# Seven products in another order, fewer loads ahead, and rearranged last rows in a hybrid decoder layer

## The chip, the cores and the metric

The kernel runs on one core of a Trainium2 chip. The metric is the device time of one execution in microseconds (us), the median of several runs. The engines are TensorE (PE; PEld is its weight load), VectorE (DVE), ScalarE (ACT), GpSimd (POOL) and SyncE (SP), which here only issues DMAs. Each engine works through a queue of its own in order; semaphores order them among each other.

## What is computed

A decoder layer on 1024 tokens of width 1024, in float32. First comes a token-mixing sub-layer (attention and a gated recurrence, one output projection), which the change doesn't touch. Then comes the channel-mixing sub-layer, which is more than half of the time:

```python
h = rmsnorm(x, pre_w_mlp[l]) * (1.0 + sc2) + sh2
u = jnp.square(jax.nn.relu(h @ w_up[l]))          # 1024 x 4096
x = x + g2 * rmsnorm(u @ w_down[l], post_w_mlp[l])
```

sh2, sc2 and g2 are rows made from a conditioning vector. The gate row g2 times the norm weight is `gw2` in the kernel.

## The kernel before, in words

**Products.** Each float32 operand is split into a high part (a rounded copy, made by ScalarE) and a low part (the difference, made by VectorE); a product of two operands is three matmuls, high by high, high by low, low by high. Every matmul has 128 rows of weights and 512 columns.

**The up scheme.** The hidden width is cut into 32 blocks of 128; two blocks are a pair, so there are 16 pairs (`NG`). Pairs 0 and 1 are computed directly (`load_cl`, `up_cl`, lines 1250 to 1264). For pairs 2 to 15 the four quarter products are built from seven products instead of eight, numbered 1 to 7, as in Strassen's scheme. Each product needs sums of the four blocks of `w_up` (`a11`, `a12`, `a21`, `a22`; `wsum`, `whi` for the high part, `wlo` for the low part) and a factor of the tokens (`bt[n, kt]`, four tiles; 5, 6, 7 and 4 are differences, made once by `factor`, line 1021; 1, 2, 3 and 8 are the tokens themselves). A product is 12 matmuls (`prod`, line 1114). Products 1, 6, 7 and 4 add up in one bank "a", 5 and 3 in bank "c", 2 in bank "b". Between them ScalarE copies the bank's state out (`snap`) and VectorE adds it to another bank (`merge`); a copy has to be done before the next product adds into the same bank. Then come `relu2` (two ScalarE operations) and sums of the results (`usum`), which are stored to `ud` in DRAM, since the down phase uses the same scheme.

**Order in the loop.** `up_slot(p, k)`, line 1305, writes out by hand what is issued in slot k of pair p; `ORDER_UP` has the order of products 1, 5, 4, 6, 3, 2, 7, where 4 is the one of the pair before. ScalarE, VectorE, TensorE and SP are "pinned": their instructions run in the order in which they are written. Elsewhere, and for GpSimd here, a planner chooses the order. In the first pair, p0 = 2, the factors of product 4 are made in slots 1 to 4 (line 1379). GpSimd makes sums of `w_dn` blocks for the down phase (`down_sums`, stored to `td`) and, for pairs 0 and 1, of their results (`direct_sums`); `JOBS` has one of them for each pair.

**The border.** The down phase reads a list `seq` of entries: `entry_w` (a `w_dn` block or `td`) and `entry_u` (`ud`), in turn; for each, a load by SP, a high part on ScalarE and a low part on VectorE. `load_ahead` (line 1227) issues loads up to `LEAD` = 6 entries ahead of the one in use; `pump(n)` splits the next n. In the last pair's slots 2 to 6 it splits 2, 3, 3, 3 and 3 entries (line 1387); the first two down stages (products 1 and 5 of pairs 0 to 3) have 8 entries each. The last pair's product 4 and the merge ahead of it (`u_tail`, line 1453) are done in the first down stage, between its four products of 128 tokens. Stores wait in `pend` until `flush` issues them on SP, at the start of a slot, in line with the loads. Loads take buffers in turn from two pools (`raw_`, 3, and `t_`, 5).

**The end.** In the last down group (pairs 14 and 15) the steps finish the rows of tokens one after the other: `accum` (VectorE), `square` (ScalarE), `root` (three GpSimd operations on a column of 128 sums), `gated` (times `gw2`, GpSimd), `scaled` (times the root, ScalarE), `residual` (plus x, VectorE), each at a step number given by `on`. `last_rows` (line 1548) does the last two blocks of rows, 3 and 7, of which 7 is finished last: its last half comes from the product `bx` ("pdlx"), in two halves of 256 columns.

## Time and profile before

| what | us |
|---|---|
| runs: lowest, median, highest | 1141.04, 1142.5, 1143.09 |
| the profiled execution: its own time | 1137.53 |
| its span, first to last instruction | 1135.7 |
| TensorE busy in the span | 1079.2 |
| VectorE, ScalarE, GpSimd busy | 825.6, 597.8, 411.3 |

All times of the trace are counted from the start of the span. "Idle before" is the time in which an engine had nothing to do ahead of an instruction, with what ended it; the profile infers that from semaphores. The pairs 2 to 15 of the up scheme run from 531 to 800 us, the down phase from there to 1119 us.

### The profile page before, as it was taken

How to read it: one execution, taken by the hardware profiler on the slowest of the kernel's cores; microseconds unless marked ns; L12 is line 12 of the kernel's file. 1: busy time of each engine (PE TensorE's matmuls, PEld its weight loads, DVE VectorE, ACT ScalarE, POOL GpSimd, SP SyncE). 2: the span in 40 equal slices, each digit the busy share in tenths (PEclk: the TensorE clock that was granted, in tenths of full speed). 3: DMA queues.
4: the chain of work that ended last, by engine and by line, in shares of the span. 5: the costliest groups of instructions: out<-in, count | busy, mean ns of one | idle time of the engine just before them, and what ended most of it. 6: DMA issues, size and time to landing. Idle time of an engine off the chain costs nothing.

```text
span 1135.7 us, 16039 instructions
## 1 busy us (share of the span) xinstructions
PE 1079.2 (95%) x5392; PEld 880.9 (78%) x5392; DVE 825.6 (73%) x1337; ACT 597.8 (53%) x1232; POOL 411.3 (36%) x534
## 2 busy tenths in 40 slices
PE   4899999999999999999899999999899999999994
PEld 3788766788788788887788888888688888888873
DVE  4865777878865564549876777887767676998786
ACT  5454654264465654565555555555664543654343
POOL 3444221134224653427555564555343000000155
PEclk9899999999999999999999999999999999999997
DMA  9700400634410343314688787777998565986554
GB/s 340 265 10 1 149 1 2 194 114 130 131 57 1 120 150 111 121 66 144 223 265 279 256 288 257 261 256 248 328 379 280 194 213 181 315 267 203 166 172 162
DMA packets 104259, 207.30 MB, mean 183 GB/s; under 512 B 13808, under 2 KB 14576, under 8 KB 104176
## 3 DMA queue, kind: packets, MB, share of 16 engines
q1 hardware_dynamic: 90288, 161.18, 41.9%
q0 software_dynamic: 13600, 44.58, 11.8%
q8 instruction: 42, 0.69, 0.2%
q10 hardware_dynamic: 288, 0.52, 0.1%
q14 instruction: 41, 0.34, 0.1%
HBM read 151.17 MB, written 55.05 MB: 182 GB/s over the span
## 4 chain that ended last, share of the span: by engine, by line
PE 78%; DVE 8%; DMA 5%; ACT 4%; POOL 3%; issue 2%; SPq 0%; DVEq 0%; POOLq 0%; ACTq 0%
PE pda L39 14%; PE pua L39 13%; PE po L39 7%; PE pdc L39 7%; PE puc L39 6%; PE pdb L39 3%; PE pv L39 3%; PE phg L39 3%; PE phq L39 3%; PE pub L39 3%; PE pq L39 3%; PE phf L39 3%; PE pu L39 2%; DMA wa<-wada 2%; PE pk L39 1%
## 5 line engine op out<-in xcount | busy, mean ns | idle before, releaser
L39 POOL TENSOR_TENSOR b<-b,b 128x512 f32<-128x512 f32 x64 | 98.8, 1544 | 81.0 <-DMA b<-w_dn 80.4
L39 ACT ACTIVATE dw<-dwr 128x512 fp32r<-128x512 f32 x72 | 45.3, 629 | 46.7 <-DMA dwr<-td 26.0
L39 ACT ACTIVATE s<-s 128x512 f32<-128x512 f32 x84 | 53.0, 631 | 31.0 <-DVE s L39 29.6
L1441 POOL DMA_DIRECT2D b<-b_g x2 | 1.1, 540 | 187.7 <-DVE acc L39 187.5
L39 DVE TENSOR_TENSOR acc<-pda,acc 128x512 f32<-128x512 f32 x68 | 46.7, 687 | 25.3 <-PE pda L39 24.2
L39 DVE TENSOR_TENSOR dw<-dwr,dw 128x512 fp32r<-128x512 f32 x72 | 55.2, 766 | 2.2 <-ACT dw L39 2.2
L39 POOL DMA_DIRECT2D b<-w_dn x64 | 34.5, 541 | 47.2 <-DMA td<-b 44.3
L39 POOL DMA_DIRECT2D td<-b x64 | 35.9, 562 | 21.6 <-POOL b L39 18.7
L39 DVE TENSOR_TENSOR wt<-a,wt 128x512 fp32r<-128x512 f32 x42 | 40.1, 955 | 0.0
L39 ACT ACTIVATE s<-pua 128x512 f32<-128x512 f32 x28 | 16.7, 597 | 42.2 <-PE pua L39 30.0
L39 PE MATMUL pua<-bt_0h,wt 128*128 128x512 f32 x84 | 32.9, 392 | 4.2 <-ACT s L39 4.2
L39 ACT ACT_TABLE_LOAD x28 | 35.9, 1283 | 0.5
L39 DVE SCALAR_TENSOR_TENSOR macc<-wada,cs,macc 128x512 f32<-128x512 f32 x42 | 33.6, 799 | 2.3 <-DMA wada<-wada 1.7
L39 DVE TENSOR_TENSOR acc<-pdc,acc 128x512 f32<-128x512 f32 x36 | 24.8, 688 | 13.5 <-PE pdc L39 13.0
L39 POOL TENSOR_TENSOR comb<-comb,rd 128x512 f32<-128x512 f32 x8 | 11.7, 1459 | 63.3 <-DVE rd L39 44.2
L39 DVE TENSOR_TENSOR wt<-s,wt 128x512 fp32r<-128x512 f32 x42 | 33.4, 794 | 0.7 <-ACT wt L39 0.6
L39 PE MATMUL pua<-bt_1h,wt 128*128 128x512 f32 x84 | 32.7, 389 | 0.0
L39 PE MATMUL pua<-bt_2h,wt 128*128 128x512 f32 x84 | 32.7, 389 | 0.0
L39 PE MATMUL pua<-bt_3h,wt 128*128 128x512 f32 x84 | 32.7, 389 | 0.0
L39 PE MATMUL pda<-dw,du_6h 128*128 128x512 f32 x96 | 29.8, 392 | 1.1 <-DVE acc L39 1.1
L39 ACT ACTIVATE wt<-s 128x512 fp32r<-128x512 f32 x42 | 26.3, 627 | 7.7 <-DVE s L39 7.5
L39 PE MATMUL pdc<-dw,du_3h 128*128 128x512 f32 x96 | 29.7, 390 | 0.2 <-DVE acc L39 0.2
(751 smaller groups left out, 3816.9 us busy)
## 6 DMA issues: line engine op xcount, KB each, us to landing
dur<-ud SPq DMA_DIRECT2D x112, 256.0 KB, 3.5
wada<-wada SPq DMA_DIRECT2D x64, 256.0 KB, 3.2
b<-w_dn POOLq DMA_DIRECT2D x64, 256.0 KB, 4.3
td<-b POOLq DMA_DIRECT2D x64, 256.0 KB, 3.3
dwr<-td SPq DMA_DIRECT2D x64, 256.0 KB, 3.6
a<-w_u SPq DMA_DIRECT2D x56, 256.0 KB, 4.4
dwr<-w_dn SPq DMA_DIRECT2D x48, 256.0 KB, 3.8
ud<-s SPq DMA_DIRECT2D x42, 256.0 KB, 3.9
```

What stands on the lines that cost most here:

```text
L39: ins = op(*args, **kw)
L1441: nc.gpsimd.dma_start(b5, I["b_g2"][hs[half]].partition_broadcast(P))
```

## The change

In the first pair the order of products becomes 1, 2, 5, 6, 3, (none), 7, and its product 4 is done after product 3 of the next pair. The loads and splits for its products 1 and 2 are written earlier; the factors of product 4 are made in slots 3 to 6, sums, high parts and low parts each a slot after the other. GpSimd is pinned in the loop too, with `direct_sums` first. The first 16 entries of `seq` are loaded 4 ahead instead of 6, and the last pair's slots 5 and 6 split 1 and 0 entries instead of 3 and 3. At the end, `root` becomes one VectorE and one GpSimd operation; the factor sqrt(D) that the root then lacks is put into `gw2`, whose multiplication goes to VectorE. `scaled` and `residual` move up one and two steps for rows 0, 1, 4 and 5; for rows 2 and 6 one fused operation on VectorE (`final`) does both. In `last_rows` the order of the last operations changes, and row 7's gated halves get tiles of their own (`gl`).

```diff
+    def factor_sum(n, kt):
         b11, b12, b21, b22 = raws[kt][0], raws[kt][1], raws[kt + 4][0], raws[kt + 4][1]
         dst, x, y = {5: (b11, b12, b11), 6: (b11, b22, b11), 7: (b12, b22, b12), 4: (b21, b21, b11)}[n]
         DVE.tensor_tensor(dst, x, y, ALU.subtract)
-        bt[n, kt] = split(dst, m_ if n == 4 else hT_, f"bt{n}_{kt}")
+        fraw[n, kt] = dst
+
+    def factor_hi(n, kt):
+        mk = m_ if n == 4 else hT_
+        fhl[n, kt] = hi, lo = mk(f"bt{n}_{kt}h", dt=F32R), mk(f"bt{n}_{kt}l", dt=F32R)
+        ACT.activation(hi, fraw[n, kt], AF.Copy)
+
+    def factor_lo(n, kt):
+        bt[n, kt] = hi, lo = fhl.pop((n, kt))
+        DVE.tensor_tensor(lo, fraw.pop((n, kt)), hi.bitcast(F32), ALU.subtract)
...
-        while at["load"] < min(len(seq), at["use"] + LEAD + 1):
+        while at["load"] < min(len(seq), at["use"] + (LEAD if at["load"] >= 16 else 4) + 1):
...
+    p0 = CL // 2
+    aload(p0, "a11", "a12", "a21", "a22")
+    whi(p0, 1)
+    wlo(p0, 1)
     for f in range(4):
         up_cl(f, 1)
-    p0 = CL // 2
     factors(5)
-    aload(p0, "a21", "a22", "a11", "a12")
+    whi(p0, 2)
+    wlo(p0, 2)
...
-    JOBS = [(down_sums, k) for k in range(4)] + [(direct_sums, k) for k in range(2)]
-    JOBS += [(down_sums, k) for k in range(4, 12)]
+    JOBS = [(direct_sums, k) for k in (1, 0)] + [(down_sums, k) for k in range(12)]
...
-        n = ORDER_UP[k]
+        n = ORDER_UP[k] if old else (1, 2, 5, 6, 3, None, 7)[k]
+        k4 = 4 if o == p0 else 2
         flush()
-        if k == 2:
-            if old:
-                prod(o, 4)
-        else:
+        if n and (k != 2 or not old):
             prod(p, n)
+        if old and k == k4:
+            prod(o, 4)
...
-    pin(True, ACT, DVE, PE, SP)
+    pin(True, ACT, DVE, POOL, PE, SP)
     for p in range(p0, NG):
         for k in range(7):
             up_slot(p, k)
-            if p == p0 and 1 <= k <= 4:
-                factor(4, k - 1)
+            if p == p0 and k >= 3:
+                for kt in (2 * k - 6, 2 * k - 5):
+                    if kt < 4:
+                        factor_sum(4, kt)
+                    if 2 <= kt < 6:
+                        factor_hi(4, kt - 2)
+                    if kt >= 4:
+                        factor_lo(4, kt - 4)
...
-                pump((0, 0, 2, 3, 3, 3, 3)[k], ends[1])
+                pump((0, 0, 2, 3, 3, 1, 0)[k], ends[1])
...
-                POOL.tensor_tensor(gw2[:, hs[half]], gw2[:, hs[half]], g5[half][3], ALU.mult)
+                DVE.scalar_tensor_tensor(gw2[:, hs[half]], gw2[:, hs[half]], float(D ** 0.5), g5[half][3], ALU.mult, ALU.mult)
...
+    def root_of(r, part, a, b):
+
+        DVE.tensor_scalar(part, a, b, D * EPS, ALU.add, ALU.add)
+        POOL.tensor_tensor(r, part, mhalf[:, 0:1], ALU.pow)
...
-                for j, hf in ((4, 1 - half), (5, half)):
+                for j, hf in ((3, 1 - half), (4, half)) if t < 2 else ():
                     on(step + j, lambda tb=tb, hf=hf: scaled(tb, hf))
-                for j, hf in ((6, 0), (7, 1)):
+                for j, hf in ((4, 0), (5, 1)) if t < 2 else ():
                     on(step + j, lambda tb=tb, hf=hf: residual(tb, hf))
...
+        def final(tb, half):
+            if (tb, 0) not in xs:
+                xs[tb, 0], xs[tb, 1] = take(), take()
+            DVE.scalar_tensor_tensor(accs[tb][half], accs[tb][half], rr_[tb][:, 0:1], xs[tb, half], ALU.mult, ALU.add)
+            store(tb, half)
...
         add(accs[b][1], ba)
+        sq(accs[b][1], ss[:, 0:1])
         add(accs[b][0], ba)
         root(a)
         gated(a, 1)
-        sq(accs[b][1], ss[:, 0:1])
-        scaled(a, 0)
-        for step in range(nstep + 3, max(later, default=0) + 1):
-            rest(step)
-        xa = [take(), take()]
...
-        DVE.tensor_tensor(accs[b][0], accs[b][0], gw2[:, h[0]], ALU.mult)
-        POOL.tensor_scalar(one["t"], ss[:, 2:3], one["part"][:, 0:1], 1.0 / D, ALU.add, ALU.mult)
-        POOL.tensor_tensor(one["r"], one["t"], mhalf[:, 0:1], ALU.pow)
-        DVE.tensor_tensor(accs[a][0], accs[a][0], xa[0], ALU.add)
+        DVE.tensor_tensor(gl[1], accs[b][1], gw2[:, h[1]], ALU.mult)
+        DVE.tensor_scalar(one["part"], ss[:, 0:1], ss[:, 1:2], D * EPS, ALU.add, ALU.add)
+        DVE.tensor_tensor(gl[0], accs[b][0], gw2[:, h[0]], ALU.mult)
+        DVE.tensor_tensor(one["part"], one["part"], ss[:, 2:3], ALU.add)
+        POOL.tensor_tensor(one["r"], one["part"], mhalf[:, 0:1], ALU.pow)
+        final(6, 1)
+        xa = [take(), take()]
+        for half in range(2):
+            scaled(a, half)
+            POOL.tensor_tensor(accs[a][half], accs[a][half], xa[half], ALU.add)
+        for half in range(2):
+            DVE.scalar_tensor_tensor(gl[half], gl[half], one["r"][:, 0:1], take(), ALU.mult, ALU.add)
+            (nc.scalar if half else nc.sync).dma_start(out[b * P:(b + 1) * P, h[half]], gl[half])
         store(a, 0)
+        final(6, 0)
```

## Rows read from the trace of the kernel before

**Rows 1.** The page: busy time of each engine, and two of its costliest groups.

```profile
PE 1079.2 (95%) x5392; PEld 880.9 (78%) x5392; DVE 825.6 (73%) x1337; ACT 597.8 (53%) x1232; POOL 411.3 (36%) x534
...
L39 ACT ACTIVATE dw<-dwr 128x512 fp32r<-128x512 f32 x72 | 45.3, 629 | 46.7 <-DMA dwr<-td 26.0
...
L39 DVE TENSOR_TENSOR dw<-dwr,dw 128x512 fp32r<-128x512 f32 x72 | 55.2, 766 | 2.2 <-ACT dw L39 2.2
```

**Rows 2.** What TensorE waited for, 470 to 1136: total us, times, longest.

```profile
PE pua L39 <- DVE s L39: 4.5, 1, 4.5
...
PE pua L39 <- ACT s L39: 4.2, 2, 2.4
...
PE pda L39 <- DVE acc L39: 1.3, 3, 0.7
```

**Rows 3.** Stretches: us, busy PE, PEld, DVE, ACT, POOL, clock, DMA share, GB/s.

```profile
835.00:1090.00 255.00, 254.05 (x1119) 209.45 (x1117) 201.15 (x312) 123.07 (x205) 21.89 (x26) 1.00 0.71 234
...
800.00:805.00 5.00, 5.00 (x24) 3.99 (x23) 4.30 (x8) 2.63 (x5) 1.76 (x3) 1.00 1.06 399
...
811.00:815.00 4.00, 4.00 (x11) 3.13 (x12) 3.66 (x4) 3.03 (x6) 2.76 (x3) 0.57 0.98 345
```

**Rows 4.** Timeline of TensorE, first pair: start, duration, [idle before <- releaser].

```profile
531.04 0.39 PE L39 MATMUL pua<-bt_0h,wt 128*128 128x512 f32 x1
...
533.76 0.39 PE L39 MATMUL puc<-bt_0h,wt 128*128 128x512 f32 x1
...
538.42 0.50 PE L39 MATMUL pua<-bt_0h,wt 128*128 128x512 f32 x1 [1.78 <-ACT s L39]
...
541.97 0.50 PE L39 MATMUL puc<-bt_0h,wt 128*128 128x512 f32 x1 [0.54 <-ACT s L39]
...
550.12 0.50 PE L39 MATMUL pua<-bt_0h,wt 128*128 128x512 f32 x1 [2.42 <-ACT s L39]
```

**Rows 5.** Timeline of the other engines ahead of and in the first pair.

```profile
521.12 2.26 DVE L39 TENSOR_TENSOR h<-h,h 128x512 f32<-128x512 f32 x1
...
521.52 1.30 POOL L39 TENSOR_TENSOR b<-b,b 128x512 f32<-128x512 f32 x1
...
548.96 0.63 ACT L39 ACTIVATE bt_2h<-h 128x512 fp32r<-128x512 f32 x1 [4.41 <-DVE h L39]
```

**Rows 6.** Timeline of SP, VectorE and TensorE at the border of the phases.

```profile
792.84 0.33 SPq L39 DMA_DIRECT2D dwr<-w_dn  x1
...
800.70 0.69 DVE L39 TENSOR_TENSOR us<-a,us 128x512 f32<-128x512 f32 x1 [4.88 <-DMA ud<-s]
...
808.07 1.00 DVE L39 TENSOR_TENSOR du_5l<-dur,du_5h 128x512 fp32r<-128x512 f32 x1 [1.87 <-ACT du_5h L39]
...
810.20 0.68 DVE L39 TENSOR_TENSOR s<-pua,s 128x512 f32<-128x512 f32 x1
...
810.93 0.50 PE L39 MATMUL pua<-bt_0h,wt_4h 128*128 128x512 f32 x1 [4.46 <-DVE s L39]
...
815.39 0.62 PE L39 MATMUL pda<-dw,du_1h 128*128 128x512 f32 x2
```

**Rows 7.** The chain that ended last, at the border: start, us, what.

```profile
793.23 7.03 DMA ud<-s
```

**Rows 8.** Timeline of all engines after the last product.

```profile
1118.24 0.40 PE L39 MATMUL pdlx<-dw,du_4h 128*128 128x256 f32 x2
...
1121.27 1.95 ACT L39 ACTIVATE acc<-acc,r_f 128x512 f32<-128x512 f32 x3 [2.40 <-POOL r_f L39]
...
1124.46 0.42 DVE L39 TENSOR_TENSOR acc<-pdlx,acc 128x256 f32<-128x256 f32 x1
...
1127.87 0.56 POOL L39 TENSOR_TENSOR l_r<-l_t,mhalf 128x1 f32<-128x1 f32 x1
...
1128.40 1.26 POOL L39 TENSOR_TENSOR acc<-acc,x 128x512 f32<-128x512 f32 x1
...
1128.46 2.41 DVE L39 SCALAR_TENSOR_TENSOR acc<-acc,l_r,x 128x512 f32<-128x512 f32 x2 [0.73 <-POOL l_r L39]
```

More of the change, by code (lines that the diff above doesn't have):

```diff
@@ L1019, in second_raw @@
             bt[n, kb % 4] = (hi, lo)
-    def factor(n, kt):
+    fraw, fhl = {}, {}
+    def factor_sum(n, kt):
         b11, b12, b21, b22 = raws[kt][0], raws[kt][1], raws[kt + 4][0], raws[kt + 4][1]
@@ L1024, in factor @@
         DVE.tensor_tensor(dst, x, y, ALU.subtract)
[L1025 removed]
+        fraw[n, kt] = dst
[6 more added lines that the diff above has]
+        DVE.tensor_tensor(lo, fraw.pop((n, kt)), hi.bitcast(F32), ALU.subtract)
     def factors(n):
         for kt in range(4):
[L1029 removed]
+            factor_sum(n, kt)
+            factor_hi(n, kt)
+            factor_lo(n, kt)
     for tb in range(5):
@@ L1290, in hybrid_layer @@
     wsum(p0, 6)
-    for n in (6, 2):
-        whi(p0, n)
-        wlo(p0, n)
+    whi(p0, 6)
+    wlo(p0, 6)
     wsum(p0, 3)
@@ L1330, in up_slot @@
         elif k == 2:
-            snap(p, "c", "s5")
             if old:
+                snap(p, "c", "s5")
                 usum(o, 5)
@@ L1339, in up_slot @@
             aload(q + 1, "a22")
-            if old:
+            if old and k4 == 2:
                 relu2_a12(o)
                 usum(o, 6)
+            elif not old:
+                snap(p, "c", "s5")
             if more:
@@ L1354, in up_slot @@
                 wsum(q, 6)
-            if old:
+            if old and k4 == 2:
                 usum(o, 3)
@@ L1359, in up_slot @@
         elif k == 5:
+            if old and k4 == 4:
+                relu2_a12(o)
+                usum(o, 6)
+                usum(o, 3)
             merge(p, "c", "s2")
@@ L1496, in gated @@
         POOL.tensor_tensor(accs[tb][half], accs[tb][half], gw2[:, half * 512:half * 512 + 512], ALU.mult)
+    def root_of(r, part, a, b):
+        DVE.tensor_scalar(part, a, b, D * EPS, ALU.add, ALU.add)
+        POOL.tensor_tensor(r, part, mhalf[:, 0:1], ALU.pow)
     def root(tb):
-        ss = small.tile([P, 1], F32, tag="ss1", name=f"ssf{tb}")
-        POOL.tensor_tensor(ss, ssr[tb][:, 0:1], ssr[tb][:, 1:2], ALU.add)
-        rr_[tb] = rstd_of(ss, D, 1, f"f{tb}")
+        ss, rr_[tb] = (small.tile([P, 1], F32, tag=f"{n}1", name=f"{n}f{tb}") for n in ("ss", "rr"))
+        root_of(rr_[tb], ss, ssr[tb][:, 0:1], ssr[tb][:, 1:2])
     def scaled(tb, half):
@@ L1550, in last_rows @@
         ss = small.tile([P, 3], F32, tag="ssl", bufs=1, name="ssl")
-        one = {n: small.tile([P, 1], F32, tag="l_" + n, bufs=1, name="l_" + n) for n in ("part", "t", "r")}
+        one = {n: small.tile([P, 1], F32, tag="l_" + n, bufs=1, name="l_" + n) for n in ("part", "r")}
         h = [slice(0, 512), slice(512, D)]
         ba, bc, bb, bx = bk["a", 3], bk["c", 3], tp_ps("pdlb"), tp_ps("pdlx")
+        gl = [m_(f"gl{half}") for half in range(2)]
         def sq(acc, col, w=512):
@@ L1580, in last_rows @@
         gated(a, 1)
-        sq(accs[b][1], ss[:, 0:1])
-        scaled(a, 0)
-        for step in range(nstep + 3, max(later, default=0) + 1):
-            rest(step)
-        xa = [take(), take()]
+        assert not later
         for i in range(2):
@@ L1588, in last_rows @@
             sq(acp[i], ss[:, 1 + i:2 + i], 256)
-            if i == 0:
-                DVE.tensor_tensor(accs[b][1], accs[b][1], gw2[:, h[1]], ALU.mult)
-                POOL.tensor_scalar(one["part"], ss[:, 0:1], ss[:, 1:2], D * EPS, ALU.add, ALU.add)
-        DVE.tensor_tensor(accs[b][0], accs[b][0], gw2[:, h[0]], ALU.mult)
-        POOL.tensor_scalar(one["t"], ss[:, 2:3], one["part"][:, 0:1], 1.0 / D, ALU.add, ALU.mult)
-        POOL.tensor_tensor(one["r"], one["t"], mhalf[:, 0:1], ALU.pow)
-        DVE.tensor_tensor(accs[a][0], accs[a][0], xa[0], ALU.add)
+        DVE.tensor_tensor(gl[1], accs[b][1], gw2[:, h[1]], ALU.mult)
[11 more added lines that the diff above has]
+            (nc.scalar if half else nc.sync).dma_start(out[b * P:(b + 1) * P, h[half]], gl[half])
         store(a, 0)
-        scaled(a, 1)
-        POOL.tensor_tensor(accs[a][1], accs[a][1], xa[1], ALU.add)
+        final(6, 0)
         store(a, 1, nc.scalar)
-        for half in range(2):
-            acc = accs[b][half]
-            DVE.scalar_tensor_tensor(acc, acc, one["r"][:, 0:1], take(), ALU.mult, ALU.add)
-            store(b, half, nc.scalar if half else nc.sync)
     last_rows()
```

9 lines of the change are left out of this document (5 added, 4 removed).

## The prediction

> **What bounds the kernel now.** I began with the page's busy times: TensorE works 95% of the span, everything else far less [rows 1]. So time can only be lost where TensorE waits or where it has already ended, and the second view is who TensorE waited for from the up scheme on. The reader is to see three things there: one wait of 4.5 us for VectorE, two of the three waits of the first pair (together 4.2 us) for ScalarE, and a rest of 1.3 us in the last group [rows 2]. Third, the stretches: from 835 to 1090 TensorE is busy 254.05 of 255.00 us at full granted clock, so what is won ahead of it is kept through it, as long as its feeders keep up: VectorE is busy 201 of those 255 us [rows 3]. That leaves three places: the first pair (A), the border between the phases (B), and the end after the last product (C).
>
> **A, the first pair.** One product takes 2.72 us (533.76 - 531.04). The starts of products 6, 3 and 7 lie 4.66, 3.55 and 8.15 us after the start before them that the rows show, where 2.72, 2.72 and 5.44 (product 2 lies in between) would do: lost are 1.94 + 0.83 + 2.71 = 5.48 us [rows 4]. Each time the wait is for ScalarE's copy ("snap") of the bank into which the product adds. For product 7 the copy stands behind the split of a factor of product 4, and ScalarE waited 4.41 us for VectorE's sum of that factor [rows 5]. VectorE is the one that is late: in this stretch its sums share time with GpSimd's, and one took 2.26 us while a sum of GpSimd's (1.30 us) ran, where such an operation takes 0.68 us elsewhere (the pua merge of rows 6) [rows 5, 6].
>
> The change takes away the cause of each: the order 1, 2, 5, 6, 3, 7 puts two products instead of one between product 1 and product 6, one between 5 and 3 as before, but with nothing of product 4's factors ahead of the copies, and one between 6 and 7. Product 4's factors (four sums, four copies, four differences, the same count) go to slots 3 to 6, and each copy is issued a slot after its sum, so that ScalarE no longer stands in wait for it. Product 4 itself goes into the next pair, two products later than before; TensorE's count is the same. The splits for products 1 and 2 come from loaded blocks alone and go ahead of the factors: no new work. Their four loads are moved past the stores of the classical blocks on SP; no row here prices that, so 0, with bounds of 0 and one landing at the border's slow rate, 7.03 us [rows 7], and I take 0, because products 1 and 2 need a block and a factor of the tokens, and no sum. The new order puts the copy for product 3 behind two splits for the next pair on ScalarE (0.63 us each [rows 1]), which hang on one sum of VectorE: the cover is product 6 (2.72 us).
>
> GpSimd's jobs: direct sums first, the rest after them, and all in written order. This moves GpSimd's sums away from the factors and into the pairs behind, where TensorE never waits [rows 2]. Each collision costs VectorE 2.26 - 0.68 = 1.58 us, and nothing of it reaches the path while VectorE has room; 0, bounds one collision either way (-1.6 to +1.6). GpSimd is busy 36% of the span [rows 1], and its results are wanted in the down phase, some 270 us later (down products begin just ahead of 806.5). I take 5.0 of the 5.48 us: a third of a collision is left.
>
> **B, the border.** TensorE idles 4.46 us ahead of the last pair's product 4, waiting for VectorE's merge at 810.20; and its twelve matmuls then take 815.39 - 810.93 = 4.46 us, not 2.72, at a granted clock of 0.57, between the two levels 1.2 and 2.4 GHz: it had idled just before [rows 3, 6]. B costs 4.46 + 1.74 = 6.20 us. The merge is late because VectorE stood 4.88 us at a sum that needs a buffer, and the buffer is freed by a store that SP issued at 793.23, behind a load that it could not issue before 792.84 for want of a free buffer [rows 6, 7]; then 1.87 us for a split of a late load [rows 6]; and because the splits of five entries that could come later stand ahead of the merge, at 0.77 us each (3.9 us) [rows 1]. Together 4.88 + 1.87 + 3.9 = 10.6 us: without them the merge could be ready at 799.6, and it is then bound by the last product 7, which ends two products (5.4 us) ahead of 806.5, where the idle time begins. The change takes out both causes: four loads ahead, not six, so that stores pass, and 9 entries, not 14, ahead of the merges. Even if the 4.88 us stall stayed, the merge would start 5.8 us ahead of 810.20, at 804.4, and end ahead of 806.5. I take the whole 6.20; the lower bound is 0 (first rival). What is late next is the five moved entries: together with two that were left anyway, seven entries of product 5 now have four products and product 4 (13.6 us) to arrive and be split. A load takes 7.03 us at this place [rows 7], its split 0.63 and 0.77 [rows 1], 8.4 in all; with five in flight that is 1.7 us each, 11.8 for seven. It fits, with little to spare, and DMA is at a share of 1.06 there [rows 3].
>
> Here a rule of the Trainium skill speaks against the change: DMA: Bandwidth & Descriptors, Rules for kernel authors, says to issue a transfer early and wait for it late, so that its fixed cost is hidden. The rows show early loads that hold back a store behind them, so at this place the trace goes against it. By the rule alone B would gain nothing and the result would be the first rival's.
>
> **C, the end.** The last matmul is over at about 1118.6 (1118.24 + 0.40) [rows 8]. Its half-row is added only at 1124.46, since VectorE stands behind sums that wait for three scalings of ScalarE (from 1121.27), which wait 2.40 us for a root on GpSimd [rows 8]. The last two fused operations end at 1128.46 + 2.41 = 1130.87; 4.8 us of closing follow, which nobody touches. After the change VectorE has two full adds ahead (0.7 each, the first begins when product 7 is over, just before 1118.24), so from about 1119.5 it does two half adds (0.42 each); then row 3's root on GpSimd (estimated to end at 1120.2 from the same adds) is followed by a gating of 1.26, till about 1121.5, beside which the first of two gate multiplies (0.7 each) waits: 1122.9. Two tiny additions on VectorE have no row; between 0 and 0.42 (the half add), taken at 0.2 in sum; the root, now one GpSimd operation of 0.56 [rows 8]: 1123.6. Then three fused operations on VectorE and two sums of 1.26 us on GpSimd. Beside such a sum two fused operations took 2.41 us [rows 8], against 1.4 without; if both sums collide, 3 x 0.7 + 2 x 1.26 = 4.6 us: 1128.2, a gain of 2.7. Bounds: no collision, 1125.7 and a gain of 5.2; or the operations moved to VectorE eat it up, 0. I take 2.7, since the row shows the collision.
>
> **Small edits with one answer.** The gate row's two multiplies go from GpSimd to VectorE, in a stretch where TensorE waits on VectorE (1.3 us [rows 2]): two fused operations more (0.7 to 1.2 each), two GpSimd sums that collide less: 0, bounds -1.2 to +1.6. Scaling and sums of rows 0, 1, 4, 5 one or two steps earlier: the same work, 0, bounds one wait of 0.7 either way [rows 2].
>
> **Sum.** 5.0 + 6.2 + 2.7 = 13.9 us. Against the profiled execution (1137.53, span 1135.7): 1123.6, span 1121.8. The median of the runs shown is 5.0 above the profiled one; I take the gain to be the same there: 1142.5 - 13.9 = **1128.6**.
>
> **The rivals.** First, B turns into a wait for loads. If only three loads are in flight, the seven entries take 7 x 8.4/3 = 19.7 us against 13.6: 6.1 us are given back, 1134.7. For it: the share of 1.06. Against it: the ring of load buffers is as large as before, and the change delays loads and adds none.
> Second, A moves on. VectorE has as many sums as before in these two pairs; if GpSimd's direct sums collide three times more (4.7 us), products 3 or 6 of the second pair wait: 1128.6 + 5.0 = 1133.6. Against it: rows 2 have no wait in the later pairs, where VectorE does the same sums beside GpSimd's.
> Third, C does not do what it says: the order on VectorE changes, but the last fused operations wait for GpSimd's queue: 1131.3.
> The other side: the first rival's mechanism with no more than two loads in flight. Then seven entries take 29.5 us and TensorE waits 15.9 us in product 5 of the first down stage, more than all three gains: 1144.5, slower. It decides at 13.6 + 13.9 = 27.5 us for the seven, or 3.9 us each. Against it: rows 7 has the slowest landing of the stretch, and it is not yet the rule.
>
> **How the numbers follow.** Forecast 0.62, first rival 0.15, second 0.10, third 0.05, two of them and more together (no change) 0.03, the other side 0.05. Within 0.2% (2.3 us, about what a measurement of this kernel can tell from no change) lies only the fifth: 0.03, and 0.02 of the others. Faster 0.90, same 0.05, slower 0.05. The range: at the low end all bounds of A and B and 4 us at C, 1142.5 - 5.5 - 6.2 - 4.0 - 2 = 1124.8, taken as 1124.5; at the high end the first rival with its own small bounds, 1136. Outside lie the last two cases and the corners.
>
> **What would show it.** A right: no TensorE wait above 0.3 us between the first product 1 and the second pair's product 7. B right: TensorE starts the last product 4 right behind the second down product, at a granted clock of 1.00, and VectorE has no wait for a store of ud. C right: the half-row's add starts within 1.5 us of the last matmul, and about 9.5 us from there to the last fused operation, not 12.2. Wrong: TensorE waits for a split of du or dw behind the border (first rival and the other side), or waits for "s" in pair two (second).

## The result, and the profile after

| kernel | median us | lowest to highest | runs |
|---|---|---|---|
| before | 1142.79 | 1141.04 to 1143.09 | 4 |
| after | 1126.06 | 1125.90 to 1126.31 | 4 |

The ratio is 0.9857, 95% interval 0.984 to 0.9874: 16.3 us faster (14.4 to 18.3). The forecast was 13.9 us and 1128.6; its 1142.5 for the kernel before is the median of three of these four runs. The two profiled executions stand only 11.55 apart (1137.53 and 1125.98). So the sum of the prediction lies between two measured gains that differ by 5 us. About 1 us of the 5 is the choice of runs: 23 more runs of before, beside the first four experiments, have a median of 1141.3, and against them the gain is 15.2 us. The questions are where the rest is, and which edit brought what.

The page of the changed kernel: TensorE's busy time is 4.4 us less, in a span 11.5 us shorter.

```profile
PE 1074.8 (96%) x5392; PEld 878.7 (78%) x5392; DVE 817.5 (73%) x1347; ACT 593.6 (53%) x1228; POOL 403.5 (36%) x517
```

What TensorE waited for from 470 to 1125 (total us, times, longest):

```profile
PE pda L39 <- DVE acc L39: 2.6, 4, 1.3
PE pu L39 <- POOL bt_1l L39: 0.5, 1, 0.5
PE pu L39 <- ACT rl L39: 0.2, 1, 0.2
PE pdc L39 <- DVE acc L39: 0.2, 1, 0.2
```

Beside [rows 2] the reader sees the wait of 4.5 us at the border and the 4.2 us of the first pair gone, and the wait for VectorE's add in the last group grown from 1.3 to 2.6 us.

The border, first TensorE and VectorE in order of time, then two stretches (us, busy PE, PEld, DVE, ACT, POOL, clock, DMA share, GB/s):

```profile
795.95 0.69 DVE L39 TENSOR_TENSOR s<-pua,s 128x512 f32<-128x512 f32 x1 [1.27 <-PE pua L39]
...
801.19 0.39 PE L39 MATMUL pua<-bt_0h,wt_4h 128*128 128x512 f32 x1
...
803.91 0.62 PE L39 MATMUL pda<-dw,du_1h 128*128 128x512 f32 x2
```

```profile
800.00:805.00 5.00, 5.00 (x23) 4.14 (x23) 4.74 (x5) 4.54 (x9) 3.76 (x5) 1.00 0.47 166
811.00:815.00 4.00, 4.00 (x19) 3.32 (x18) 3.39 (x6) 3.65 (x8) 1.63 (x3) 1.00 1.06 407
```

The merge now waits for the last product 7, ends at 796.64 and lies 4.55 us ahead of product 4, which takes 2.72 us (803.91 - 801.19) at the full granted clock; in [rows 6] the merge began only at 810.20, and the product took 4.46. In the second stretch DMA is at a share of 1.06, which the first rival was built on, and TensorE waits for nothing there.

To compare all kernels stretch by stretch, I counted TensorE's matmuls, 5392 in each, and took the time between the starts of the same ones. "Beginning" runs from the start of the span to the 2881st, in the first pair's second product; "pairs 2 and 3" to the 3101st, with all of the first two pairs' waits; "later pairs" to the 4001st; "border" to the 4121st; "down" to the 5201st; "last group" to the last matmul's start; "end" from there to the end of the span. The columns add up to the span of the profiled execution, which is read to 0.1 us, so that the last column is good to 0.05.

| kernel | beginning | pairs 2 and 3 | later pairs | border | down | last group | end |
|---|---|---|---|---|---|---|---|
| before | 535.12 | 55.79 | 204.00 | 33.64 | 244.80 | 45.13 | 17.22 |
| before, a second profile | 536.99 | 55.67 | 204.00 | 37.63 | 244.80 | 45.13 | 17.27 |
| A alone | 533.88 | 49.87 | 204.00 | 35.50 | 244.80 | 45.13 | 17.23 |
| B alone | 536.88 | 56.11 | 204.00 | 27.20 | 244.80 | 45.13 | 17.27 |
| C alone | 537.33 | 55.69 | 204.00 | 36.06 | 244.80 | 46.47 | 15.85 |
| **after** | 535.99 | 49.87 | 204.00 | 27.20 | 244.80 | 46.49 | 15.85 |

From before to after, profile to profile: A 5.92, B 6.44, C 1.37 - 1.36 = 0.01, which is nothing within that 0.05, and a beginning that was 0.87 longer: 11.50. A's earlier loads and splits lie in the beginning, but no effect of them is seen: over all fourteen profiles it takes 533.88 to 537.37 us with them and 535.12 to 537.33 without. Where no edit touches them, the later pairs and the down phase agree to 0.01 us and the last group to 0.02; pairs 2 and 3 scatter by 0.4 (55.67 to 56.11), the beginning by some 3 us, and the border of the kernel before by 4.

### The profile page after: what moved, and what is told of

It reads as the page before. It is cut to its first block, busy times and chain, and to the rows that moved or that the text cites. A ratio compares the mean times of both kernels' runs of the same rounds, so it can differ in the third digit from the quotient of the medians.

```text
span 1124.2 us, 16031 instructions
## 1 busy us (share of the span) xinstructions
PE 1074.8 (96%) x5392; PEld 878.7 (78%) x5392; DVE 817.5 (73%) x1347; ACT 593.6 (53%) x1228; POOL 403.5 (36%) x517
## 4 chain that ended last, share of the span: by engine, by line
PE 78%; DVE 8%; POOL 4%; ACT 4%; issue 3%; DMA 3%; DVEq 0%; SPq 0%; POOLq 0%; ACTq 0%
PE pua L39 14%; PE pda L39 13%; PE pdc L39 7%; PE puc L39 7%; PE po L39 6%; PE pu L39 4%; PE pdb L39 3%; PE pub L39 3%; PE pq L39 3%; PE pv L39 3%; PE phg L39 2%; PE phq L39 2%; PE phf L39 2%; DVE acc L39 2%; PE pk L39 2%
## 5 line engine op out<-in xcount | busy, mean ns | idle before, releaser
L39 POOL TENSOR_TENSOR b<-b,b 128x512 f32<-128x512 f32 x64 | 90.6, 1416 | 214.2 <-DMA b<-w_dn 213.9
L39 DVE TENSOR_TENSOR dw<-dwr,dw 128x512 fp32r<-128x512 f32 x72 | 52.2, 725 | 8.3 <-ACT dw L39 8.3
L39 DVE TENSOR_TENSOR acc<-pda,acc 128x512 f32<-128x512 f32 x68 | 46.4, 683 | 15.2 <-PE pda L39 15.0
L39 DVE TENSOR_TENSOR wt<-s,wt 128x512 fp32r<-128x512 f32 x42 | 39.7, 946 | 0.9 <-ACT wt L39 0.8
L39 POOL TENSOR_TENSOR acc<-acc,gw 128x512 f32<-128x512 f32 x14 | 20.3, 1456 | 30.6 <-ACT fin L39 30.6
L39 DVE TENSOR_TENSOR s<-puc,s 128x512 f32<-128x512 f32 x14 | 9.7, 690 | 29.4 <-issue 27.2
L39 DVE TENSOR_TENSOR wt<-a,wt 128x512 fp32r<-128x512 f32 x42 | 30.3, 721 | 0.0
```

The source lines that it names most:

```text
L39: ins = op(*args, **kw)
```

## The experiments

**The kernel before once more.** Nothing is edited; it asks whether the 5 us between its profile and its median stand in one place.

> The kernel before, unchanged, for a second profiled execution. Theory 1 (the first profiled execution, 1137.53, was an unusually quick one; the runs without a profile are the rule): the second profiled execution lies near the median, 1141 to 1143, and its extra 4 to 5 us stand in one place of the trace, as a longer wait of TensorE. Theory 2 (a profiled execution of this kernel is always quicker than an unprofiled one): 1137 to 1138 again, with the same waits: 4.5 us for the last pair's product 4 and 4.2 us in the first pair.

Measured: 1141.32 median (1138.25 to 1143.30, 12 runs); the profiled execution took 1143.30. Its border, VectorE and TensorE in order of time, and one stretch:

```profile
804.87 1.37 DVE L39 TENSOR_TENSOR du_1l<-dur,du_1h 128x512 fp32r<-128x512 f32 x1 [3.07 <-ACT du_1h L39]
...
815.27 0.68 DVE L39 TENSOR_TENSOR s<-pua,s 128x512 f32<-128x512 f32 x1
...
816.00 0.79 PE L39 MATMUL pua<-bt_0h,wt_4h 128*128 128x512 f32 x1 [6.49 <-DVE s L39]
```

```profile
816.00:821.00 5.00, 5.00 (x12) 3.93 (x13) 5.00 (x5) 4.63 (x9) 3.76 (x4) 0.51 0.78 283
```

The border cost 37.63 - 27.20 = 10.43 us here, 6.44 in the first profile: theory 1, though only 4 of the 5.8 us between the two executions are the border's, the rest the beginning's. And the wait on which the prediction built its cause is not there: VectorE's sum that stood 4.88 us for a store of ud in [rows 6] did not wait at all. Instead it waited 3.07 us for a late load's split, 1.56 and 1.48 for two more, and TensorE waited 2 us longer (6.49), with a granted clock of 0.51 in the stretch behind the wait. Which transfer comes late differs from run to run; that fourteen entries and their loads stand ahead of the merge does not.

**A alone.** The whole of the first pair's edits and GpSimd's jobs, on the kernel before:

```diff
+        n = ORDER_UP[k] if old else (1, 2, 5, 6, 3, None, 7)[k]
...
-    JOBS = [(down_sums, k) for k in range(4)] + [(direct_sums, k) for k in range(2)]
-    JOBS += [(down_sums, k) for k in range(4, 12)]
+    JOBS = [(direct_sums, k) for k in (1, 0)] + [(down_sums, k) for k in range(12)]
...
-    pin(True, ACT, DVE, PE, SP)
+    pin(True, ACT, DVE, POOL, PE, SP)
```

> The kernel before with part A alone: the first pair's order, its factors and splits, and GpSimd's jobs in the new written order. Theory 1 (as predicted, independent parts): 5.0 to 5.5 us faster than before, no wait in the first pair, and the wait of 4.5 us at the border as before. Rival (A moves on: what TensorE gains is lost again in the later pairs or at the border, where the same VectorE work now meets GpSimd's sums): 0 to 2 us faster, with a new wait behind the first pair. Rival 2 (the jobs of GpSimd that A moves also ease the border): over 7 us faster, and a border wait under 3 us.

Measured: 1131.88, ratio 0.9912 (0.9896 to 0.9927), 10 us (9.4 by medians). In its profile the first pairs gain 5.92, no wait is left there, and the border keeps a wait of 5.17 us (35.50). Rival 1 is out: nothing moved on. Ten microseconds by the timed runs against 5.92 in the stretch point to rival 2, an easier border; but the one profile doesn't show that.

**B alone.**

```diff
-        while at["load"] < min(len(seq), at["use"] + LEAD + 1):
+        while at["load"] < min(len(seq), at["use"] + (LEAD if at["load"] >= 16 else 4) + 1):
...
-                pump((0, 0, 2, 3, 3, 3, 3)[k], ends[1])
+                pump((0, 0, 2, 3, 3, 1, 0)[k], ends[1])
```

> The kernel before with part B alone: four loads ahead for the first sixteen entries, and 1 and 0 entries instead of 3 and 3 in the last two slots. Theory 1: 6.2 us faster, no wait ahead of the last pair's product 4, granted clock 1.00 there. Rival (the border's loss is larger in runs without a profile than in the profiled one, and is where the 5 us between the two lie): 9 to 11 us faster by the timed runs. Rival 2 (load ring): under 2 us faster, with waits for splits of du or dw in the first down stage.

Measured: 1132.65, ratio 0.9914 (0.9899 to 0.9930), 9.8 us (8.7 by medians): about the rival's size. The border falls to 27.20, as in the changed kernel, and no wait of the load ring appears.

**C alone.** The end and the gate row:

```diff
+        DVE.tensor_scalar(part, a, b, D * EPS, ALU.add, ALU.add)
+        POOL.tensor_tensor(r, part, mhalf[:, 0:1], ALU.pow)
...
-        POOL.tensor_tensor(ss, ssr[tb][:, 0:1], ssr[tb][:, 1:2], ALU.add)
-        rr_[tb] = rstd_of(ss, D, 1, f"f{tb}")
...
-                for j, hf in ((6, 0), (7, 1)):
+                for j, hf in ((4, 0), (5, 1)) if t < 2 else ():
```

> The kernel before with part C alone: the end and the gate row. In the trace of the changed kernel the stretch from the last matmul to the last fused operation is 10.7 us against 12.1 before, and there is a new wait of 1.28 us for VectorE's add in the last group. Theory 1: so C is worth 1.4 less about 0.9 for the new wait, 0.5 us, by the profile: 0 to 1 us faster. Rival (C as predicted, the new wait belongs to the other parts): 2.0 to 2.7 us faster.

Measured: 1140.05, ratio 0.9983 (0.9968 to 0.9998), which the border's scatter blurs. The table is sharper: the end is 1.37 us shorter, the last group 1.34 longer. C is worth nothing, and its new wait is its own, since neither A nor B alone has it.

By the ratios the three parts add to 10.0 + 9.8 + 1.9 = 21.7 us, but together they bring 16.3; by medians against the same 23 runs, 9.4 + 8.7 + 1.3 = 19.4, and together 15.2. So some 4 to 5 us are saved by more than one part, most likely by A and B at the border (see the end of the next section).

**B without the smaller lead**, on the changed kernel:

```diff
-        while at["load"] < min(len(seq), at["use"] + (LEAD if at["load"] >= 16 else 4) + 1):
+        while at["load"] < min(len(seq), at["use"] + LEAD + 1):
```

> The changed kernel with six loads ahead at the border again; the 1 and 0 entries of the last two slots stay. The changed kernel took 1126.06. Theory 1 (either edit of B alone is enough, as the prediction said: with the stall kept the merge still ends ahead of 806.5): 1126 to 1127.5, no wait ahead of the last pair's product 4. Theory 2 (SP's queue carries the loss: a store stands behind loads that find no free buffer): 1130 to 1134, and VectorE waits for a store of ud or a late load, TensorE 3 us or more.

Measured: 1127.22 (1125.66 to 1127.37). The border is 27.20, to the digit that of the changed kernel; its profiled execution is 1.4 us longer in the beginning (537.37), which the edit doesn't touch. With the entries moved, four loads ahead instead of six are worth nothing.

**B without the moved entries**, on the changed kernel:

```diff
-                pump((0, 0, 2, 3, 3, 1, 0)[k], ends[1])
+                pump((0, 0, 2, 3, 3, 3, 3)[k], ends[1])
```

> The changed kernel with 3 and 3 entries in the last two slots again; four loads ahead stay. Theory 1 (either edit alone is enough): 1126 to 1127.5, no wait ahead of product 4. Theory 2 (the entries carry the loss: whatever delays the loads, fourteen entries ahead of the merges hold these up): 1130 to 1134, with a wait of 3 us or more for VectorE's merge and VectorE waiting for splits of late loads.

Measured: 1130.54 (1128.80 to 1132.15). VectorE and TensorE at its border:

```profile
797.05 0.69 DVE L39 TENSOR_TENSOR du_5l<-dur,du_5h 128x512 fp32r<-128x512 f32 x1 [2.10 <-ACT du_5h L39]
...
803.66 0.68 DVE L39 TENSOR_TENSOR s<-pua,s 128x512 f32<-128x512 f32 x1
...
804.39 0.80 PE L39 MATMUL pua<-bt_0h,wt_4h 128*128 128x512 f32 x1 [2.94 <-DVE s L39]
```

The border costs 33.31, 6.1 us more than in the changed kernel, and VectorE waits for splits of late loads, not for a store. Theory 2: the entries carry B, and the smaller lead doesn't rescue it. Whether it helps by a microsecond or two where fourteen entries stand there, the border's scatter hides (A alone, with six ahead, lost 8.3).

**Two loads ahead**, on the changed kernel; the prediction's other side:

```diff
-        while at["load"] < min(len(seq), at["use"] + (LEAD if at["load"] >= 16 else 4) + 1):
+        while at["load"] < min(len(seq), at["use"] + (LEAD if at["load"] >= 16 else 2) + 1):
```

> The changed kernel with two loads ahead for the first sixteen entries, not four: the prediction's other side, tried. By the prediction's sum for two in flight (seven entries in 29.5 us against 13.6) TensorE would wait 15.9 us in the first down stage: 1142. By three in flight (19.7 us): 1132. Rival (loads land in about 4.5 us, the page's median, so the entries come at least every 2 us): 1126 to 1128, no wait for splits of du or dw.

Measured: 1126.67 (1126.30 to 1127.05). The border stays 27.20, and the first down stages lose nothing. The down phase is 1.11 us longer (245.91), but all of it from 978 to 985 us, behind one wait of 0.46, some 170 us after the sixteen entries that the edit holds back; nothing shows that the edit caused it. The 15.9 us that the prediction priced don't appear, though not because loads land sooner: from 788 to 812 us they take 3.3 to 8.7 us here (medians 6.1 and 6.2). The run doesn't test two loads in flight either. The lead is counted in entries of the written order, and in time up to six of these loads are in flight at once (at 796.64, for one), as in the changed kernel.

**GpSimd's jobs as before**, on the changed kernel:

```diff
-    JOBS = [(direct_sums, k) for k in (1, 0)] + [(down_sums, k) for k in range(12)]
+    JOBS = [(down_sums, k) for k in range(4)] + [(direct_sums, k) for k in range(2)] + [(down_sums, k) for k in range(4, 12)]
...
-    pin(True, ACT, DVE, POOL, PE, SP)
+    pin(True, ACT, DVE, PE, SP)
```

> The changed kernel with GpSimd's jobs as before: the old order of direct and down sums, and free of the written order. The prediction put this part at 0, with bounds of one collision either way (-1.6 to +1.6). Theory 1: 1126 to 1127.7, at most one short wait in the first two pairs. Rival 1 (GpSimd's sums beside VectorE's are what made the copies late, and the order of products only moved that): 1129 to 1132, with waits for ScalarE's copies in the first pair again. Rival 2 (the jobs' order acts at the border, through GpSimd's transfers beside SP's loads): no wait in the first pair, but one at the border.

Measured: 1129.69 (1128.62 to 1129.83), and 53.11 us in pairs 2 and 3 where the changed kernel has 49.87. Its VectorE and GpSimd in the first pair, then TensorE in the second:

```profile
546.77 1.45 POOL L39 TENSOR_TENSOR b<-b,b 128x512 f32<-128x512 f32 x1 [0.59 <-DMA b<-w_dn]
...
547.00 3.96 DVE L39 TENSOR_TENSOR h<-h,h 128x512 f32<-128x512 f32 x2
...
549.10 1.30 POOL L39 TENSOR_TENSOR b<-b,b 128x512 f32<-128x512 f32 x1
...
556.49 0.50 PE L39 MATMUL pua<-bt_0h,wt 128*128 128x512 f32 x1 [2.02 <-ACT s L39]
...
560.03 0.50 PE L39 MATMUL puc<-bt_0h,wt 128*128 128x512 f32 x1 [0.49 <-ACT s L39]
```

The same operations in the changed kernel:

```profile
541.74 2.97 POOL L39 TENSOR_TENSOR xe<-xc,xe 128x512 f32<-128x512 f32 x1 [4.15 <-DMA xe<-ud]
...
542.26 1.29 DVE L39 TENSOR_TENSOR h<-h,h 128x512 f32<-128x512 f32 x2
```

Two sums of VectorE take 3.96 us beside two of GpSimd's; they take 1.29 where a single sum of GpSimd falls into a row of VectorE's that has begun (and it is GpSimd's that is stretched then, to 2.97). The time is that of the expectation's rival 1, the place is not: without the new jobs the new order of products leaves no wait in the first pair and 2.51 us of waits for the copies in the second. That is where the prediction's second rival put them, but the sums that collide are down sums (`b`), not direct sums. The new jobs are what keeps these waits away.

**The new list of jobs, free of the written order**, on the changed kernel:

```diff
-    pin(True, ACT, DVE, POOL, PE, SP)
+    pin(True, ACT, DVE, PE, SP)
```

> The changed kernel with GpSimd's jobs in the new list (direct sums first) but free of the written order, as before. With the old list and free, the first two pairs took 53.1 us, with the new list and the written order 49.9. Theory 1 (the list decides: direct sums wait for transfers between one another, so they come singly, where down sums come three in a row): 49.9 us and 1126 to 1127. Theory 2 (the written order decides: free, GpSimd begins its jobs before the pairs and runs beside the factors): 52 to 53 us, 1128 to 1130, with a wait for ScalarE's copies.

Measured: 1125.86 (1125.50 to 1126.10); 50.45 us in pairs 2 and 3. The list decides, not the written order: it brings 2.66 of the 3.24 us. But theory 1's reason doesn't hold. Free of the written order the direct sums don't all come singly (two of one job follow at 534.19 and 536.36 without a wait between them), and VectorE loses more time beside GpSimd in the 20 us from the first pair's first product on than in any other kernel: 6.14 us, counted over 0.69 for each 128x512 operation, against 1.81 in the changed kernel. What the kernels with the new list share lies ahead of the pair. GpSimd in the kernel before, then in this run:

```profile
516.74 1.72 POOL L39 TENSOR_TENSOR b<-b,b 128x512 f32<-128x512 f32 x1 [3.16 <-DMA b<-w_dn]
...
519.34 1.30 POOL L39 TENSOR_TENSOR b<-b,b 128x512 f32<-128x512 f32 x1
```

```profile
527.61 1.30 POOL L39 TENSOR_TENSOR xa<-xa,xc 128x512 f32<-128x512 f32 x1 [2.40 <-DMA xc<-ux]
```

The old list puts three sums (the third in [rows 5]) beside VectorE's factors, before the first product at 531.04; the new list's first sum waits for a load of the direct pairs' results. In the 25 us ahead of that product VectorE loses 6.27 to 6.29 us by the same count in the five profiles with the old list, and 3.05 to 3.14 in the nine with the new one. That the list acts through these 3.2 us is likely, not shown: no run separates them from the rest of it.

**The jobs alone**, on the kernel before: the same two lines as in A alone, JOBS and the pin, with the old order of products.

```diff
-    JOBS = [(down_sums, k) for k in range(4)] + [(direct_sums, k) for k in range(2)]
-    JOBS += [(down_sums, k) for k in range(4, 12)]
+    JOBS = [(direct_sums, k) for k in (1, 0)] + [(down_sums, k) for k in range(12)]
...
-    pin(True, ACT, DVE, PE, SP)
+    pin(True, ACT, DVE, POOL, PE, SP)
```

> The kernel before with GpSimd's jobs alone changed (new list, written order); order of products and factors as before. The first two pairs took 55.8 us before, 53.1 with the new order of products alone, 49.9 with both. Theory 1 (the two add up: each takes away its own delay of VectorE or ScalarE): 52.5 us, a gain of 3.2 in this stretch. Theory 2 (the jobs' part only keeps the gain from moving into the second pair): 55 to 56 us, no gain without the order. Theory 3 (the collisions with GpSimd were the whole cause): 50 to 51 us, and the order of products is worth nothing beside it. At the border: a mean loss under that of before (9 us or so by the timed runs) if the jobs ease it.

Measured: 1132.42 (1128.73 to 1134.61), ratio 0.9922 (0.9896 to 0.9947). What TensorE waited for:

```profile
PE pua L39 <- DVE s L39: 2.5, 1, 2.5
...
PE pua L39 <- ACT s L39: 0.9, 1, 0.9
```

Pairs 2 and 3 take 51.21: 4.58 of A's 5.92 us without any change in the order of products, nearest theory 3. The order adds 1.34. The border is 31.63, the shortest of any kernel with fourteen entries there.

**The end changed again**, on the changed kernel: roots of rows 0, 1, 4, 5 wholly on GpSimd, their last sums one step later, and the last rows' scaling and sums as fused operations of VectorE alone. Row 3's root moves behind a gate multiply, and its last store goes from ScalarE's queue to SP's.

```diff
-        DVE.tensor_scalar(part, a, b, D * EPS, ALU.add, ALU.add)
+        eng.tensor_scalar(part, a, b, D * EPS, ALU.add, ALU.add)
...
-                for j, hf in ((4, 0), (5, 1)) if t < 2 else ():
+                for j, hf in ((5, 0), (6, 1)) if t < 2 else ():
...
-        for half in range(2):
-            scaled(a, half)
-            POOL.tensor_tensor(accs[a][half], accs[a][half], xa[half], ALU.add)
+        final(6, 0)
+        final(a, 0)
+        final(a, 1)
```

> The changed kernel with the end changed again: the roots of rows 0, 1, 4, 5 wholly on GpSimd, their last sums one step later, and the last rows finished by fused operations of VectorE alone (no scaling on ScalarE, no sum on GpSimd beside them), row 3's gating ahead of its root. Theory (VectorE's written order makes the new wait of 1.28 us: the add that frees TensorE's bank stands behind a last sum of 1.18 and a wait of 0.53 for a square): the last group 45.1 to 45.7 us, not 46.5, and the end, from the last matmul's start, 14.5 to 15.2 us, not 15.85; in all 1124 to 1125. Rival 1: the wait comes from the gate row's multiplies on VectorE or from the add's own place: 46.5 stays. Rival 2: without GpSimd's share VectorE is the longer one at the end: 16 us or more.

Measured: 1119.53 (1119.45 to 1119.84), ratio to before 0.9813 (0.9797 to 0.9828); 6.5 us faster than the changed kernel. The last group takes 44.83 and the end 10.97. The gate row's multiplies are where they were, so rival 1 is out, and so is rival 2. VectorE and GpSimd at the end:

```profile
1105.24 4.20 POOL L39 TENSOR_TENSOR acc<-acc,gw 128x512 f32<-128x512 f32 x3
...
1105.39 1.69 DVE L39 SCALAR_TENSOR_TENSOR acc<-acc,rrf,x 128x512 f32<-128x512 f32 x1
1107.01 1.27 DVE L39 TENSOR_TENSOR acc<-pda,acc 128x512 f32<-128x512 f32 x2
...
1110.83 2.73 DVE L39 SCALAR_TENSOR_TENSOR acc<-acc,rrf,x 128x512 f32<-128x512 f32 x4
1111.21 0.76 POOL L39 TENSOR_TENSOR l_r<-l_part,mhalf 128x1 f32<-128x1 f32 x1
1113.48 1.40 DVE L39 SCALAR_TENSOR_TENSOR gl<-gl,l_r,x 128x512 f32<-128x512 f32 x2
```

Six fused operations without a sum of GpSimd beside them take 4.05 us (1110.83 to 1114.88); in the changed kernel four of them took 5.26. The last of them ends 7.75 us after the last matmul's start, not 10.98: 3.2 us of the 4.88 that the end gains, 1.45 of it because the half-row's adds begin sooner (1.25 us after that start, not 2.70). The other 1.7 come after the last fused operation, where no work but the last stores is left: 4.88 us in the changed kernel, 3.19 here. That the end gave some 4 us more than was expected lies in these parts.

**One tiny operation behind the end.** In all thirteen profiles up to there the span ended 6.1 us after GpSimd's last operation. So this was tried:

```diff
+        last = small.tile([P, 1], F32, tag="l_last", bufs=1, name="l_last")
+        POOL.tensor_tensor(last, gl[1][:, 0:1], mhalf[:, 0:1], ALU.add)
```

> The version with the end changed again, with one tiny operation of GpSimd (128x1) added behind the last fused operation; its result is used by nothing. In the profiles of all kernels so far the span ends 6.1 us after GpSimd's last operation, whatever VectorE and the last stores do: 4.88 us after VectorE's last operation where GpSimd ended late, 3.19 where it ended early. Theory 1 (GpSimd's last operation sets the end of the span): the tiny operation ends about 0.7 us after the last fused one, so the end, from the last matmul's start, is 7.75 + 0.7 + 6.1 = 14.5 us, not 10.97, and the time 1123. Theory 2 (the last store's landing sets it, and the 6.1 us are chance): 11.0 to 11.2 us, 1119.5 to 1120.

```profile
1114.13 1.40 DVE L39 SCALAR_TENSOR_TENSOR gl<-gl,l_r,x 128x512 f32<-128x512 f32 x2
...
1115.60 0.19 POOL L39 TENSOR_TENSOR l_last<-gl,mhalf 128x1 f32<-128x1 f32 x1 [2.98 <-DVE gl L39]
```

Measured: 1123.79 (1123.01 to 1124.32), 4.3 us more than without it, for an operation of 0.19 us that nobody waits for. In the profiles 3.14 of it stand in the end, which took 14.11 us instead of 10.97 with VectorE's part the same, and 0.7 in the beginning, which scatters. The span ends at 1121.9, 6.1 us after the tiny operation. So theory 1 holds: where GpSimd's last operation comes late, it sets the end of the span.

## Why the prediction was right, and where it was not

The direction was right and the time lay in the range. That the sum came out only 2.5 us off is in part luck, since mis-sized terms of both signs met: against the 15.2 us of more runs, A brought 0.9 us more than was taken, B some 3.1 more (by difference), C 2.7 less; the other 1.2 us are the starting point, 1142.5 against 1141.3. By its own steps:

**A: 5.0 predicted, 5.92 measured; the credit was wrong.** That VectorE is late because its sums share time with GpSimd's was read correctly from [rows 5], and no wait is left up to the second pair's product 7, as the test asked. But the step that set GpSimd's jobs to 0, within one collision (1.6 us) either way, failed. The jobs alone bring 4.58 us, the order of products alone 55.79 - 53.11 = 2.68 (with C and B beside it, which don't touch the stretch), both 5.92. The argument was that nothing of a collision reaches the path "while VectorE has room", in a stretch whose every wait was for an engine held up by VectorE: the cause that the paragraph above it had just named. The second rival, at 0.10, has the place of the waits that come without the jobs, but not their cause. The 5.92 are also 0.44 more than the 5.48 that the prediction found lost: it stopped at the start of product 7, and the products behind that start were slower too (5.59 us for the next two, 555.71 - 550.12, not 5.44).

**B: 6.20 predicted, 6.44 measured in the profile on which the sum was made, 10.43 in the next one.** The cost of idle time and slow product was right, and so was "bound by the last product 7". Three steps failed. First, the stall for a store behind a load was taken for a cause; it was one of several forms of late transfers, and absent where the loss was largest. Second, the smaller lead was counted as half of the cure: the entries alone do (27.20 with six loads ahead), as the sentence "even if the 4.88 us stall stayed" had it, but the lead alone leaves 33.31. Third, the gain of one profiled execution was carried over to the median, and [rows 6] turned out to hold the smallest of the border's losses without B: 6.44, 10.43, and 8.86 in C alone. That is where most of the difference between the gain of 11.55 and that of 15.2 must stand: with C at zero, 1141.3 - 1126.06 - 5.92 leaves 9.3 us for the border, 2.9 more than in the profile, and 0.87 are the beginning's.

**The rivals of B** (load ring, three or two in flight, 0.20 together) rested on the 7.03 us of [rows 7] as the landing of every load. That row is a store (`ud<-s`), and it is not the slowest of its stretch, as the prediction said: the loads issued right behind it, from 794.28 to 797.27, landed after 6.9 to 7.6 us, so the size was about right for that place. What failed is the number in flight: not two or three, but up to six in the changed kernel, with the same landings (2.9 to 7.1 us from 788 to 812). No wait for a split appears behind its border.

The rule of the Trainium skill that the prediction set aside (DMA: Bandwidth & Descriptors, Rules for kernel authors: issue early, wait late) is not refuted by [rows 6, 7], though I wrote that the trace goes against it there. Issuing less early brought nothing (27.20 at the border with six, four and two ahead); no run here shows a loss by it either. What the changed kernel does is wait later.

**C: 2.7 predicted, 0.01 measured.** The third rival's result, at 0.05, and only in a small part by its mechanism: the last fused operations wait 0.44 us for GpSimd's root. The end of the changed kernel, with VectorE and GpSimd after TensorE's last matmul, in order of time:

```profile
1107.92 2.95 POOL L39 TENSOR_TENSOR acc<-acc,gw 128x512 f32<-128x512 f32 x2
1108.07 1.68 DVE L39 SCALAR_TENSOR_TENSOR acc<-acc,rrf,x 128x512 f32<-128x512 f32 x1
1108.35 0.28 PE L39 MATMUL pdlx<-dw,du_4l 128*128 128x256 f32 x1
1109.67 1.28 DVE L39 TENSOR_TENSOR acc<-pda,acc 128x512 f32<-128x512 f32 x2
1111.05 0.76 DVE L39 TENSOR_TENSOR acc<-pdlx,acc 128x256 f32<-128x256 f32 x2
1111.73 1.81 POOL L39 TENSOR_TENSOR acc<-acc,gw 128x512 f32<-128x512 f32 x1
1112.45 1.63 DVE L39 TENSOR_TENSOR gl<-acc,gw 128x512 f32<-128x512 f32 x1
1114.07 0.74 DVE L39 SCALAR_TENSOR_TENSOR acc<-acc,rrf,x 128x512 f32<-128x512 f32 x1
1115.19 2.92 POOL L39 TENSOR_TENSOR acc<-acc,x 128x512 f32<-128x512 f32 x2
1115.26 3.41 DVE L39 SCALAR_TENSOR_TENSOR gl<-gl,l_r,x 128x512 f32<-128x512 f32 x2 [0.44 <-POOL l_r L39]
1118.59 0.74 DVE L39 SCALAR_TENSOR_TENSOR acc<-acc,rrf,x 128x512 f32<-128x512 f32 x1
```

The half-row's add starts 2.4 us after the last matmul's end (1111.05 against 1108.63), not within 1.5: `final(2, 0)`, a new fused operation, stands ahead of the adds on VectorE and takes 1.68 us beside GpSimd's gating. The prediction let the two adds begin when product 7 is over and forgot what is queued before them. The stretch from the last matmul's end to the last fused operation is then 10.7 us, not 9.5. And the last stretch was counted to the last fused operation, with 4.8 us of closing that "nobody touches". It came out (4.88 us), because GpSimd's last operation again ended 1.2 us ahead of VectorE's; it belongs to GpSimd's.

The small edits set at 0, with bounds of one wait of 0.7 us, gave the rest back, 1.36 us. TensorE and VectorE in the last group:

```profile
1091.09 1.18 DVE L39 TENSOR_TENSOR acc<-acc,x 128x512 f32<-128x512 f32 x1
...
1092.80 0.68 DVE L39 TENSOR_TENSOR acc<-pda,acc 128x512 f32<-128x512 f32 x1
1093.79 0.21 DVE L39 TENSOR_SCALAR ssf<-ssf 128x1 f32<-128x1 f32 x1 [0.32 <-ACT fin L39]
1093.92 0.68 DVE L39 TENSOR_TENSOR acc<-pda,acc 128x512 f32<-128x512 f32 x1
...
1094.66 0.50 PE L39 MATMUL pda<-dw_1h,du_1h 128*128 128x512 f32 x1 [1.28 <-DVE acc L39]
```

The add that frees TensorE's bank (1093.92) stands behind a last sum that the change moved up and that is stretched to 1.18 us beside GpSimd, and behind the root's first half, which the change put on VectorE and which waits there for ScalarE's square. With both moved back (the version with the end changed again) the last group takes 44.83 and the wait of 1.28 is gone; that the two together make it is shown, their shares are not.

**What stays open.** Kernels with the new list of jobs seem to lose less at the border. Counted by medians over the changed kernel, with the profiles' other stretches taken out: A alone 5.8 us, B without the moved entries 4.5, the jobs alone 1132.42 - 1126.06 - 1.34 = 5.0; without the new list 9.3 (before) and 1140.05 - 1126.06 - 5.82 = 8.2 (C alone). So the list would be worth some 3 to 4 us there as well, and this would be the time that A alone and B alone both save. It is not shown: a median also holds the beginning's scatter, and over 27.20 the single profiles overlap (8.30, 6.11 and 4.43 with the new list, 6.44, 10.43 and 8.86 without it). How the list would act there was not tried.

## What to carry to other kernels

A stall found in one profiled execution is one draw: profile the unchanged kernel twice before giving a wait a cause, and ask which work could stand later instead of which transfer came late. In an engine's written order an added operation can hold up all that stands behind it, a tiny one too when it waits for another engine; list what is queued ahead of the operation on the path before summing durations. Work on GpSimd is not free while VectorE is on the path; look for it ahead of the stretch that waits, too. At the end of a kernel look at when GpSimd finishes: here one tiny operation behind all others cost 3.1 us of the end.

## What the runs showed of the hardware that was not expected

The span ended 6.1 us (6.09 to 6.10) after GpSimd's last operation in all fourteen profiles, whether VectorE's last operation came 1.2 us after it, 2.9 us after it or 0.3 us before it; an added operation of 0.19 us lengthened the end by 3.1 us. The traces also hold instructions that the views leave out: a DRAIN of GpSimd's ends 5.3 us after its last operation (5.31 or 5.32 in the four profiles read for it: before, after and the two last versions), and the closing steps of all engines come behind it. In the version with the end changed again SP's last DRAIN, which follows the last store's landing, ends at the same moment (1117.31 against 1117.29), so by this trace GpSimd ending sooner would have brought nothing more there. Whether the 6.1 us hold where GpSimd ends much earlier was not tested.

VectorE's fused operation took 0.74 us alone and 1.68 to 1.75 beside a sum or a gating of GpSimd's, an add that reads one operand from PSUM 0.68 beside the same gating (1107.01 in the version with the end changed again, two in 1.27 us). The Trainium skill says so (SBUF — State Buffer, Who interferes with whom): a VectorE instruction with two inputs in SBUF contends with a GpSimd instruction that reads SBUF, and the order of issue decides which of the two is held up. These rows agree with it, and the 1.68 us of `final(2, 0)` could have been expected from it.

How long GpSimd is held up was not expected. In the kernel before, one of its sums, begun inside a row of VectorE's, ended only after the row:

```profile
528.00 10.35 POOL L39 TENSOR_TENSOR b<-b,b 128x512 f32<-128x512 f32 x1 [3.26 <-DMA b<-w_dn]
...
537.40 1.51 DVE L39 TENSOR_TENSOR bt_3l<-h,bt_3h 128x512 fp32r<-128x512 f32 x1 [0.17 <-ACT bt_3h L39]
```

From 525.71 to 537.23 VectorE ran operations of 0.68 us one behind the other, none of them stretched. Its first pause is the 0.17 us here, and the operation behind the pause is the first that is stretched, while GpSimd's sum ends at 538.35.
